# A hybrid state space and attention block: vector and scalar engine in program order through the state space stage

## The chip, the cores and the metric

One Trainium2 chip, one of its cores. The metric is the device time of one launch in microseconds (us), lower is better. The core's engines run side by side, each with a queue of its own: PE (TensorE, matmul; its weight loads are listed as PEld), DVE (VectorE), ACT (ScalarE), POOL (GpSimd) and SP (SyncE, which here only issues DMAs).

## The reference

One block on 512 tokens of width 1024, in float32:

```
proj = rms_norm(x) @ w_in
z, xbc, dt, q, k, v, g_ssd, g_attn = split(proj)
xbc = silu(causal_dwconv(xbc)); xs, B, C = split(xbc)       # 4 taps
# 8 groups of 4 heads of 64, state 128, chunks of 128 tokens:
y = (C B^T * decay) (xs dt) + C state_before_chunk * decay + d_skip * xs
y_ssd = rms_norm_by_group(y * silu(z))
y_attn = merge over 3 window groups by their softmax sums
merged = sigmoid(g_ssd) * (y_ssd @ w_ssd_proj) + sigmoid(g_attn) * (y_attn @ w_attn_proj)
x = x + merged @ w_out
x = x + (silu(u_gate) * u_val) @ w_down,   u = causal_dwconv(rms_norm(x) @ w_up)
```

## The kernel before

Every weight product runs in three float32r passes: the weight is split into `whi` (an ACT cast, L105) and `wlo` (a DVE subtraction, L106), the input into `hh` and `hl`, and a *piece* is 24 matmuls of 128x512 into one "mm" bank of PSUM: eight of whi·hh, eight of whi·hl, eight of wlo·hh (`mm_chan`, L140). `raw`, `whi` and `wlo` have three buffers each. PSUM has four "mm", two "tr" and two "aux" banks, each kind handed out in rotation (L61).

The stage in question has 48 pieces for the state space branch (`ps_ssd`), six for each of eight groups: B, C, two of xs, two of z; then 16 gate pieces (`ps_gate`). Between the pieces runs small work, held in *sides*: Python generators in a list (L121 to L138). A *tick* goes through the list, oldest first, and takes from each side the next portion, unless the side still waits: `yield n` means n ticks until the next portion. A piece has two ticks, one after its twelfth matmul (L148 to L150, behind a `prefetch` that makes the weight two pieces ahead) and one at its end (L815). So a group lasts twelve ticks. PE runs in the order in which the program issues (L152). For DVE and ACT, here, the framework chooses the order by a cost model of its own, and can place an instruction long before the tick that issues it. From the end of the output projection on (L1184) DVE, ACT and POOL too run in program order.

The sides are:

- `chain` (L525): attention, one per head pair, two per group of windows still running when the stage begins; the last ends at tick 9 and starts `combine` (L603), which waits eleven ticks. `combine` loads the softmax sums, forms weights `f`, transposes them (`ps_fT`, L626), copies them (`ft`, L628), sends them through DRAM, loads them back spread over partitions (`fb`), and then, for four head pairs j, does what is called a *strip* below: three products (L645) and two sums (L647) on DVE, a cast `ah` on ACT (L651), and a tick later `al` on DVE (L653).
- `conv4` (L676): the four-tap convolution of one piece out of its bank: one ACT step (L677) and three of DVE (L681, recorded as L51). It is called right after the piece, and so is the copy of z (L812).
- `silus` (L778): silu over a group's B and C, xs, or z.
- `ssd_side` (L696), one per group, with its waits from `G0`, `G1`, `GN`: the decay matrix `bc` (L705, L707, L708), the products C·B (`ps_cb`, L714, masked into `cbm`), B by token (`ps_bt`, L720, `btok`), `bc` times `cbm` (L723), xs by token (`ps_xt`, L733, twice four transposes) scaled into `xdt` and `xdc` (L736, L739), the chunk states (`ps_st`, L745) and their running sum `prev` (L750 to L754), and for each half j of the group's channels `ps_y` (L764), `ps_o` (L769) and four DVE steps that make y (L771 to L774). At its end it loads the decay of group g+2 (L685).

So PE meets a group's small matmuls in six portions: cb and bt, xt, xt, st, y and o of j = 0, y and o of j = 1. The gates' sigmoid (L836) is issued right behind its piece. Six early gates go to the buffers of the branch; `finish` (L842) runs the sides out, and POOL copies those gates into `gt` (L848), which lies where the sides' buffers were. Squares and norm sums of y follow among the gates (L856 to L876), then `normed` (L878).

## Time and profile before

| | us |
|---|---|
| median of 3 runs | 1191.93 (1191.52 to 1191.97) |
| the profiled execution | 1191.64 |
| its span, first to last instruction | 1189.9 |
| busy in it: PE, PEld | 1184.2, 988.0 |
| busy in it: DVE, ACT, POOL | 776.3, 574.5, 183.3 |

The profile is one execution. Times in its views run from the span's start; L12 is line 12 of the kernel. A row of a timeline gives start, duration, engine, line, operation, output and inputs, a count, and in brackets idle time with what ended it. A row of a list by lines gives busy time and the mean duration of one, then the idle time ahead of them. Matmuls are pipelined and their ends are modelled, so a matmul's cost is read from starts, not from durations. A busy PE is not a PE at its peak.

### The profile page before, as it was taken

What the parts mean: (1) busy time and instruction counts of PE and PEld (TensorE: products, weight loads), DVE (VectorE), ACT (ScalarE), POOL (GpSimd) and SP (SyncE); (2) the same over time, 40 slices, a digit from 0 to 9 for tenths busy, and PEclk for the clock granted to TensorE, in tenths of its full rate; (3) what the DMA queues carried; (4) which work ended last, traced back from release to release, by engine and by line L of the source; (5) the groups of instructions that cost most, each with busy time, mean ns of one, the idle gap of its engine ahead of it and who ended that gap; (6) DMA issues with size and microseconds to landing.
All of it is one profiled execution on the core that took longest, in us unless ns stands there. A gap on an engine that the chain in (4) does not pass through costs nothing.

```text
span 1189.9 us, 15865 instructions
## 1 busy us (share of the span) xinstructions
PE 1184.2 (100%) x6268; PEld 988.0 (83%) x6268; DVE 776.3 (65%) x1033; ACT 574.5 (48%) x870; POOL 183.3 (15%) x165
## 2 busy tenths in 40 slices
PE   9999999999999999999999999999999999999998
PEld 7877778987888888888887888888889898998887
DVE  6224454357789977767742374753779888888876
ACT  5434555467735655355325333432645454545443
POOL 1033432300000000000005400000133223222210
PEclk9999999999999999999999999999999999999999
DMA  5445543422645544425233523325434333249951
GB/s 189 124 112 127 127 109 91 108 55 76 183 136 176 145 124 124 142 72 142 71 85 79 173 98 100 90 89 193 143 105 125 89 107 106 80 132 279 189 123 66
DMA packets 175771, 145.24 MB, mean 122 GB/s; under 512 B 9752, under 2 KB 147848, under 8 KB 174673
## 3 DMA queue, kind: packets, MB, share of 16 engines
q1 hardware_dynamic: 167441, 127.11, 36.9%
q0 software_dynamic: 8256, 17.13, 7.3%
q8 instruction: 49, 0.80, 0.3%
q14 instruction: 25, 0.20, 0.1%
HBM read 139.51 MB, written 4.70 MB: 121 GB/s over the span
## 4 chain that ended last, share of the span: by engine, by line
PE 99%; ACT 0%; DVE 0%; issue 0%
PE ps_ssd L145 22%; PE ps_qk L145 11%; PE ps_u L1299 10%; PE ps_gate L145 7%; PE ps_sp L936 7%; PE ps_v L409 6%; PE ps_wo L969 3%; PE ps_dB L1500 3%; PE ps_ua L1125 2%; PE ps_uc L1125 2%; PE ps_ub L1125 2%; PE ps_u L145 2%; PE ps_da L1500 2%; PE ps_dc L1500 2%; PE ps_ap L145 2%; PE ps_s L537 1%
## 5 line engine op out<-in xcount | busy, mean ns | idle before, releaser
L106 DVE TENSOR_TENSOR wlo<-raw,whi 128x1024 fp32r<-128x1024 f32 x142 | 176.7, 1245 | 290.5 <-ACT whi L105 175.3
L105 ACT CAST whi<-raw 128x1024 fp32r<-128x1024 f32 x142 | 149.1, 1051 | 272.3 <-PE ps_ssd L145 75.4
L145 PE MATMUL ps_ssd<-hl,whi 128*128 128x512 f32 x384 | 102.4, 397 | 0.0
L145 PE MATMUL ps_ssd<-hh,whi 128*128 128x512 f32 x384 | 98.4, 398 | 0.0
L145 PE MATMUL ps_ssd<-hh,wlo 128*128 128x512 f32 x384 | 95.4, 390 | 0.0
L145 PEld LDWEIGHTS ps_ssd<-hh,wlo 128*128 128x128 f32 x384 | 72.1, 188 | 15.9
L145 PEld LDWEIGHTS ps_ssd<-hh,whi 128*128 128x128 f32 x384 | 70.6, 188 | 14.0 <-issue 0.2
L145 PEld LDWEIGHTS ps_ssd<-hl,whi 128*128 128x128 f32 x384 | 70.2, 188 | 13.8
L848 POOL COPY gt<-bct_gate 128x1024 f32<-128x1024 f32 x1 | 1.4, 1416 | 392.8 <-DVE ysb L773 392.8
L556 ACT ACTIVATE s<-s,st 128x128 f32<-128x128 f32 (+1 forms) x96 | 39.8, 416 | 21.6 <-DVE st L550 15.7
L1173 ACT ACTIVATE facc<-facc 128x512 f32<-128x512 f32 x22 | 13.9, 633 | 75.1 <-DVE facc L51 75.0
L145 PE MATMUL ps_qk<-hh,whi 128*128 128x512 f32 x192 | 49.3, 399 | 0.0
L1109 DVE TENSOR_TENSOR ulo<-rawup,uhi 128x1024 fp32r<-128x1024 f32 x31 | 44.6, 1437 | 5.2 <-ACT uhi L1103 5.2
L145 PE MATMUL ps_qk<-hl,whi 128*128 128x512 f32 x192 | 47.5, 389 | 0.0
L145 PE MATMUL ps_qk<-hh,wlo 128*128 128x512 f32 x192 | 47.4, 389 | 0.0
L145 PEld LDWEIGHTS ps_qk<-hh,whi 128*128 128x128 f32 x192 | 35.0, 188 | 12.1 <-issue 3.8
L1299 PE MATMUL ps_u<-h2h,uhi 128*128 128x512 f32 x176 | 43.7, 390 | 0.0
L1299 PE MATMUL ps_u<-h2l,uhi 128*128 128x512 f32 x176 | 43.5, 389 | 0.0
L1299 PE MATMUL ps_u<-h2h,ulo 128*128 128x512 f32 x176 | 43.4, 389 | 0.0
L145 PEld LDWEIGHTS ps_qk<-hl,whi 128*128 128x128 f32 x192 | 36.0, 188 | 7.6
L145 PEld LDWEIGHTS ps_qk<-hh,wlo 128*128 128x128 f32 x192 | 36.0, 188 | 7.5
L936 PE MATMUL ps_sp<-yh,whi 128*128 128x512 f32 x128 | 39.4, 389 | 0.0
(372 smaller groups left out, 2673.9 us busy)
## 6 DMA issues: line engine op xcount, KB each, us to landing
raw<-in_w_in_dram SPq DMA_DIRECT2D x100, 512.0 KB
rawup<-in_w_up_dram SPq DMA_DIRECT2D x40, 512.0 KB
bc<-scr_a SPq DMA_DIRECT2D x8, 1024.0 KB
raw<-in_w_ssd_proj_dram SPq DMA_DIRECT2D x16, 512.0 KB
c<-in_w_down_dram POOLq DMA_DIRECT2D x16, 512.0 KB, 6.3
hrb<-scr_q POOLq DMA_DIRECT2D x12, 512.0 KB, 6.5
raw<-in_w_down_dram SPq DMA_DIRECT2D x10, 512.0 KB
eb<-scr_e SPq DMA_DIRECT2D x16, 256.0 KB
```

Of the source, the lines that this page charges most:

```text
L105: nc.scalar.copy(hi, raw)
L106: marks["lo"] = nc.vector.tensor_sub(lo, raw, hi.bitcast(F32))
L145: nc.tensor.matmul(ps[:, t0:t0 + nt], a[:, k, c:c + n], b[:, k, t0:t0 + nt], start=(i == 0), stop=(i == total - 1))
L409: nc.tensor.matmul(pss[b], tok(g, kq * 2 + k, b, xx), w[:, k, :], start=(kq == 0 and j == 0 and k == 0), stop=(kq == 3 and j == 2 and k == 1))
L556: nc.scalar.activation(s[:, o:o + nk * P], s[:, o:o + nk * P], AF.Exp, bias=st[:, q, 0, 2 * j + h:2 * j + h + 1], accum_out=st[:, q, 1, 2 ...
L936: nc.tensor.matmul(pss[j], w[:, k, cs], ys[k][xi], start=(k2 == 0 and i == 0 and k == 0), stop=(k2 == 7 and i == 2 and k == 1))
L969: nc.tensor.matmul(pss[b], xs(k0 + k, i)[:, b * P:(b + 1) * P], ww[:, k, :], start=(k0 == 0 and j == 0 and k == 0), stop=(k0 == nk - 2 and ...
L1109: nc.vector.tensor_sub(lo, source(m, x), hi.bitcast(F32))
L1125: nc.tensor.matmul(ba[m][bk][:, c * H:(c + 1) * H], a[:, k, :], b[:, k, :], start=(i == 0), stop=(i == 11))
L1173: nc.scalar.activation(facc[m], facc[m], AF.Silu)
L1299: nc.tensor.matmul(pss[i], a[:, k, :], b[:, k, :], start=(n == 0), stop=(n == 23))
L1500: nc.tensor.matmul(ps, xs(j, q), w[wi][:, q, :], start=ps.name not in begun, stop=x in final and n == 5, skip_group_check=k in ("Q6", "Q3"))
```

## The change

DVE and ACT run in program order from the first state space piece to the end of the attention projection. With that the issuing program decides, and its order is written anew:

- `conv4`, the copy of z (now `keep_z`) and the sigmoid (now `sigmoid`) become sides: they begin with `yield 1` and so run at the middle of the next piece.
- `ssd_side` takes a table of the ticks of its steps, counted from the group's start: `GROUP`, and `FIRST` for group 0. `SILU` gives the ticks of the silus. A side's tick 12 is the first tick of the next group.
- A group's small matmuls go in three portions: `ps_bt`, both `ps_xt` and `ps_cb` (tick 13), `ps_st` (tick 17), `ps_y` and `ps_o` of both halves (tick 21). Their banks are four, two "tr" and two "aux". DVE and ACT work on them stands at ticks of its own. The decay of group g+2 is loaded ahead of the first half of y (tick 22).
- In `combine`, `ps_fT` takes an "mm" bank, and three ticks instead of one lie between `ah` and `al`, so a strip comes every four ticks instead of every two.
- `sq` holds one half instead of two, and `finish` is called once more after the gates.

```diff
-G0, G1, GN = (2, 1, 1, 1), (5, 2, 4, 2), (7, 2, 2)
-G2W, YL = 4, 3
+GROUP = (9, 11, 12, 13, 14, 15, 17, 18, 19, 21, 22, 23)
+FIRST = (12, 14, 15, 16, 17, 18, 19, 20, 21, 23, 24, 25)
+SILU = (8, 10, 14)
...
-        ps = bank("tr", "ps_fT")
+        ps = bank("mm", "ps_fT")
...
             nc.scalar.copy(ah[:, j, :], acc)
-            yield 1
+            yield 3
             nc.vector.tensor_sub(al[:, j, :], acc, ah[:, j, :].bitcast(F32))
...
+    ssd_cm = tc.manual_schedule(engines={mybir.EngineType.DVE, mybir.EngineType.Activation})
+    ssd_cm.__enter__()
...
     def conv4(ps, blk, acc):
+        yield 1
...
+    def keep_z(ps, o):
+        yield 1
+        nc.scalar.copy(o, ps)
...
+        waits = iter([b - a for a, b in zip(at, at[1:])])
...
         nc.vector.tensor_sub(m4, acs[:, :, hs]..., m4)
-        yield 1
+        yield next(waits)
         nc.scalar.activation(mt, mt, AF.Relu)
+        yield next(waits)
         nc.scalar.activation(mt, mt, AF.Exp, scale=-1.0)
-        yield at["cb"]
+        yield next(waits)
...
-        nc.scalar.copy(btok.rearrange("p c n -> p (c n)"), ps[:, :3 * P])
-        yield 1
-        nc.vector.tensor_mul(m4, m4, cbm.unsqueeze(1).broadcast_to((P, 4, NT, P)))
-        yield at["x"]
+        p4s = []
         for hf in range(2):
-            ps = bank("tr", f"ps_xt{g}_{hf}")
+            ps = bank(("tr", "aux")[hf], f"ps_xt{g}_{hf}")
...
+        psc = bank("aux", f"ps_cb{g}")
...
+        yield next(waits)
+        nc.scalar.copy(btok.rearrange("p c n -> p (c n)"), psb[:, :3 * P])
...
+            nc.vector.tensor_mul(xdc[:, cc], p4s[hf][:, :n], ...)
+        nc.vector.tensor_mul(cbm, psc..., triu...)
+        yield next(waits)
+            nc.vector.tensor_mul(xdt[:, cc], p4s[hf], ...)
+        yield next(waits)
...
+        yield next(waits)
+        nc.vector.tensor_mul(m4, m4, cbm.unsqueeze(1).broadcast_to((P, 4, NT, P)))
+        yield next(waits)
...
-        yield at["y"]
-        sq = T("sq", [P, 2, S])
+        yield next(waits)
+        outs = []
         for j in range(2):
-            psy = bank("aux", f"ps_y{g}_{j}")
+            psy = bank(("aux", "tr")[j], f"ps_y{g}_{j}")
...
-            pso = bank("aux", f"ps_o{g}_{j}")
+            pso = bank(("aux", "tr")[j], f"ps_o{g}_{j}")
...
+            outs.append((psy, pso))
+        sq = T("sq", [P, S])
+        for j in range(2):
+            yield next(waits)
+            if j == 0:
+                load_decay(g + 2)
...
-            yield YL - j
-        load_decay(g + 2)
...
-        if g > 1:
-            start(ssd_side(g, *tiles[g], normal), G2W if g == 2 else 0)
+            start(ssd_side(g, *tiles[g], GROUP), GROUP[0])
...
-                        conv4(banks[k], 16 + 8 * k + g, bct[:, k, :])
+                        start(conv4(banks[k], 16 + 8 * k + g, bct[:, k, :]))
...
-                        nc.scalar.copy(zs[:, k - 4, :], banks[k])
-            if i % 2 and g > 0:
-                start(silus(tiles[g][i // 2]), 1)
+                        start(keep_z(banks[k], zs[:, k - 4, :]))
+            if i % 2:
+                start(silus(tiles[g][i // 2]), SILU[i // 2] - 2 * i - 1)
...
-                start(ssd_side(0, *tiles[0], dict(zip(("cb", "x", "y"), G0))), G0[3])
-            if (g, i) == (0, 5):
-                start(ssd_side(1, *branch_tiles(1), dict(zip(("cb", "x", "y"), G1))), G1[3])
-                start(silus(*tiles[0]), 1)
+                start(ssd_side(0, *tiles[0], FIRST), FIRST[0] - 10)
+    def sigmoid(ps, o):
+        yield 1
+        nc.scalar.activation(o, ps, AF.Sigmoid)
...
-        nc.scalar.activation(o, ps, AF.Sigmoid)
+        start(sigmoid(ps, o))
         tick()
...
+    finish()
...
     nl_cm.__exit__(None, None, None)
+    ssd_cm.__exit__(None, None, None)
```

## The prediction

> **What bounds the kernel now.** The page comes first: who holds the chain of waits, and at what clock.

> ```profile
> PE 99%; ACT 0%; DVE 0%; issue 0%
> ```

> ```profile
> core 0 of [0], span 1189.9 us
> core 0: us, PE busy (x) PEld busy (x) DVE busy (x) ACT busy (x) POOL busy (x), PEclk, DMA share, GB/s
> 373.00:393.00 20.00, 20.00 (x103) 16.39 (x102) 19.75 (x33) 9.09 (x12) 0.00 (x0) 1.00 0.62 185
> 513.00:553.00 40.00, 40.00 (x215) 33.00 (x214) 29.23 (x38) 19.95 (x21) 0.00 (x0) 1.00 0.43 118
> ```

> The chain is TensorE from end to end. In both windows, which lie in the stage that changes, PE is busy throughout and the granted clock is 1.00. So the change can win only what PE itself spends, and every wait that it adds to PE is paid in full. Two windows matter: a steady group (513 to 553) leaves DVE a quarter of its time, while the stretch 373 to 393, where the merging of the three attention groups (`combine`) runs beside groups 1 and 2, fills DVE to 19.75 of 20 us. Today the scheduler spreads that work; afterwards the program does.

> Next, what PE spends on a group's small work: the timeline of PE in a steady group.

> ```profile
> 454.68 1.07 PE L145 MATMUL ps_ssd<-hl,whi 128*128 128x512 f32 x4
> 455.67 1.09 PE L764 MATMUL ps_y<-bc,xdt 128*64 128x128 f32 x16
> 456.70 0.94 PE L769 MATMUL ps_o<-bct,prev 128*128 128x128 f32 x6
> 457.39 1.17 PE L145 MATMUL ps_ssd<-hl,whi 128*128 128x512 f32 x4
> ```

> ```profile
> 462.05 1.07 PE L145 MATMUL ps_ssd<-hl,whi 128*128 128x512 f32 x4
> 462.96 1.05 PE L714 MATMUL ps_cb<-bct 128*128 128x128 f32 x8
> 463.85 0.49 PE L720 MATMUL ps_bt<-ident,bct 128*128 128x128 f32 x3
> 464.09 1.17 PE L145 MATMUL ps_ssd<-hl,whi 128*128 128x512 f32 x4
> 465.11 1.99 PE L145 MATMUL ps_ssd<-hh,wlo 128*128 128x512 f32 x8
> ```

> ```profile
> 478.78 1.46 PE L745 MATMUL ps_st<-xdc,btok 128*128 128x256 f32 x6
> 479.89 2.19 PE L145 MATMUL ps_ssd<-hh,whi 128*128 128x512 f32 x8
> ```

> Read by starts. Four piece matmuls take 0.91 us (462.05 to 462.96), 0.227 each, so a piece of 24 takes 5.44 and the half between two ticks 2.72. From 462.05 to 465.11 pass 3.06 us, of which eight piece matmuls are 1.81: the portion cb+bt costs 1.25. Its eight `ps_cb` step by 0.11 (0.89 in all), and eleven records at that step are 1.22. Going over to small matmuls and back thus costs about 0.03. The portion y+o costs 454.68 to 457.39 less 0.91, 1.80, and 0.11 for the slow four behind it (1.02 for 0.91 at 464.09): 1.9. It begins 0.08 late (455.67 for 455.59), a price of entering. The portion st costs 1.11, with its restart 1.2.

> **The change, part by part.**

> Fewer portions. A group has six today (cb+bt, two of four transposes, st, two of y+o) and then three, with the same matmuls: bt, both transposes and cb together (19 records by 0.11, 2.15 us), st, and both halves of y+o (3.8). Three borders go. At 0.03 each that is 0.1 us a group, 0.8 in all; with the entry of 0.08 saved each time too, 0.33 and 2.6. I take 1.0, near the low end, because the entry into the narrow `ps_y` tiles comes back inside the merged portion, from `ps_o` to the second `ps_y`. **Term one: minus 1.0 us (0.8 to 2.6).**

> Program order on DVE and ACT. The prices, one steady group first, then the strip of `combine` and the way that DVE instructions overlap:

> ```profile
> L106 DVE TENSOR_TENSOR wlo<-raw,whi 128x1024 fp32r<-128x1024 f32 x6 | 7.3, 1222 | 6.2 <-PE ps_ssd L145 4.4 <-ACT whi L105 1.8
> L51 DVE SCALAR_TENSOR_TENSOR xst<-ps_ssd,sc,xst 128x511 f32<-128x511 f32 (+2 forms) x6 | 4.5, 744 | 0.1
> ...
> L723 DVE TENSOR_TENSOR bc<-bc,cbm 128x2048 f32<-128x2048 f32 x1 | 2.3, 2283 | 0.0
> ...
> L51 DVE SCALAR_TENSOR_TENSOR ysb<-xst,dsk,ps_y 128x512 f32<-128x512 f32 x2 | 1.5, 744 | 0.2 <-PE ps_y L764 0.2
> L774 DVE TENSOR_TENSOR ysb<-ysb,zs 128x512 f32<-128x512 f32 x2 | 1.4, 692 | 0.1
> L736 DVE TENSOR_TENSOR xdt<-ps_xt,dtt 128x512 f32<-128x512 f32 x2 | 1.4, 692 | 4.0 <-PE ps_xt L733 4.0
> L773 DVE TENSOR_TENSOR ysb<-ysb,sq 128x384 f32<-128x384 f32 x2 | 1.1, 554 | 0.0
> L772 DVE TENSOR_TENSOR sq<-ps_o,eb 128x384 f32<-128x384 f32 x2 | 1.1, 553 | 0.1
> L739 DVE TENSOR_TENSOR xdc<-ps_xt,dtd 128x512 f32<-128x512 f32 (+1 forms) x2 | 1.1, 546 | 0.0
> L752 DVE TENSOR_TENSOR prev<-prev,cdec 128x256 f32<-128x256 f32 x2 | 0.8, 420 | 0.0
> ```

> ```profile
> L645 DVE TENSOR_TENSOR ysb<-ysb,fb 128x512 f32<-128x512 f32 x8 | 5.1, 682 | 0.0
> ```

> ```profile
> 605.96 1.23 DVE L106 TENSOR_TENSOR wlo<-raw,whi 128x1024 fp32r<-128x1024 f32 x1 [3.30 <-PE ps_gate L145]
> 607.10 0.74 DVE L51 SCALAR_TENSOR_TENSOR ysb<-xst,dsk,ps_y 128x512 f32<-128x512 f32 x1
> ```

> ```profile
> L105 ACT CAST whi<-raw 128x1024 fp32r<-128x1024 f32 x7 | 7.3, 1042 | 10.0 <-PE ps_ssd L145 10.0
> ...
> L708 ACT ACTIVATE bc<-bc 128x2048 f32<-128x2048 f32 x1 | 1.9, 1917 | 0.0
> L677 ACT ACTIVATE xst<-ps_ssd,sc 128x512 f32<-128x512 f32 x2 | 1.6, 781 | 1.6 <-PE ps_ssd L145 1.6
> ...
> L708 ACT ACT_TABLE_LOAD x1 | 1.3, 1283 | 0.0
> L812 ACT COPY zs<-ps_ssd 128x512 f32<-128x512 f32 x2 | 1.2, 576 | 0.0
> ```

> The next DVE instruction starts 1.14 us after a `wlo` of 1.23, so I take 0.09 off each that waits for nothing: `wlo` 1.14, a convolution (three of L51) 1.97, the `bc` products 2.2, a `combine` operation 0.60, so a strip (three products, two sums) 3.0 and its `al` 0.6. Chains whose members wait for each other keep full length: a half of y 2.5, `prev` (five of 0.42) 2.1.

> A steady group has room. Its tightest place is the wait of y+o (tick 21) for `prev` (tick 19): from tick 18 DVE does `wlo`, the `bc` product, a convolution and `prev`, 7.4 us, and PE takes 2.72 and 5.44, 8.2. Cost nothing; each us beyond that margin of 0.8 would cost one us in each of six groups.

> Ticks are counted from here on from group 0's first piece; group 1 begins at 12, group 2 at 24. `combine`, which wakes at tick 21, makes `ps_fT` and `ft` at 24 (after yields of 1 and 2) and its first strip at 28 (2 and 2 more).

> Ticks 24 and 25, the middle and the end of a piece. At tick 24 the oldest side, `combine`, puts its `ft` copy into DVE's queue ahead of group 0's y; `ft` waits for PE's `ps_fT`. Let group 0's y+o start on PE at 0. PE: 3.8, half a piece 2.72, four transposes 0.44, half a piece 2.72: at 9.7 it wants group 1's first portion, whose two "tr" banks hold y's second half. DVE: `ft` can start at 7.1, takes 0.6, y's first half 2.5, the first read of the second 0.74: 10.9. **Term two: plus 1.2 us**; with `ft` behind y it would be 0.

> Ticks 28 to 45: strips stand at ticks 28, 32, 36 and 40, each with an ACT copy (`ah`) that waits for it, and behind that copy ACT's convolution, silu, exp or cast, for which DVE's next instruction waits. At tick 28 DVE starts level with PE (its `wlo` needs the buffer that PE frees just then). Up to tick 35 it has five `wlo` 5.7, three convolutions 5.9, two strips 6.0, two `al` 1.2, two `bc` products 4.4, `prev` 2.1, two y halves 5.0, together 30.3, and it waits behind `ah`: once for `ah`, priced like the z copy, and the convolution's first step (0.58, 0.78, so 1.3), once for these and a silu as long as a cast (2.3). Sum 33.9. PE needs 4.5 pieces 24.5, st 1.2, y+o 3.8: 29.5. DVE is 4.4 behind at tick 36. There it does a strip (3.0), and then ACT works alone: `ah` 0.58, table load 1.28, exp 1.92, z copy 0.58, cast 1.04, 5.1 with overlaps. Only then come `wlo` 1.14, two `xdc` and `cbm` 1.5, a wait of 0.7 for ACT's table load, silu and convolution, the convolution 1.97, `al` 0.6, two `xdt` 1.2: 7.1. In all 19.6 after tick 36. PE wants group 2's st (tick 41), whose bank the second `xdt` frees, after 2.72, the first portion 2.15 and two pieces 10.88, at 15.75. **Term three: plus 3.8 us.** From there to y+o at tick 45 DVE has 1.14, 3.0, 1.3, 1.97, 1.14, 2.2, 1.97, 0.6, 2.1: 15.4; PE 1.2 and 10.88: 12.1. **Term four: plus 3.3.** Afterwards no strip is left, and DVE's quarter of spare time clears the rest.

> Bounds of these three: without overlap (0.09 on some 35 instructions) 3 us more; if the ACT-alone waits (1.3, 2.3, 5.1) were half as long, 4.3 less.

> [...]

> The rest at nothing. `ps_fT` in an "mm" bank and the later reading of banks: four banks, a bank returns three pieces (16 us) later. Later silus, sigmoids and `al`: `merged` is read only after the last gate. The loads of decay are issued at tick 22 and used eleven ticks on; on SP's queue they can hold back weight loads, of which three buffers lie ahead: 0, at worst 2 us. POOL's copies of the early gates:

> ```profile
> 619.25 1.42 POOL L848 COPY gt<-bct_gate 128x1024 f32<-128x1024 f32 x1 [392.78 <-DVE ysb L773]
> ```

> ```profile
> 632.19 1.53 POOL L848 COPY gt<-zs_gate 128x1024 f32<-128x1024 f32 x1 [9.35 <-ACT zs_gate L836]
> ```

> Their release, group 7's last y, comes some ten us later, about 629, and the third copy waits for its sigmoid until 632 anyway; beyond that the norm sums on PE would wait one for one.

> **Sum.** The profiled execution took 1191.64 us, its span 1189.9 and 1.7 around it, 0.3 below the median 1191.93. 1191.64 − 1.0 + 1.2 + 3.8 + 3.3 = 1198.9 us.

> **Rivals.** *No new wait (1190.6, not slower).* PE stays gapless and only term one is left. For it: today's trace does the same DVE work in 373 to 393 without a PE gap. Against: there strips slip in between other work; in program order each strip's `ah` holds ACT. It holds if DVE is under 0.5 us behind at tick 36. Chance 0.22. *One stall only (about 1193.5):* DVE starts tick 28 ahead, or the 5.1 overlap with work; terms two and a part of three remain, plus 1 to 3. Chance 0.15. *Faster (1188.5):* all borders are worth 0.4 us a group, 8 × 0.4 = 3.2; it needs the merged portion to shed entry, exit and the step from y to o as well. Chance 0.06. *A tax in every group (1205):* the margin of 0.8 is gone, say 1 us in six groups on top of the forecast; the steady group's 29.23 of 40 speaks against it. Chance 0.07. That DVE and ACT are not held to program order would look like the first.

> **Numbers.** Forecast (1195 to 1203) 0.50. From 1190.2 to 1203 lie the forecast, the single stall and most of the first rival, 0.83. A measurement of this kernel tells 0.2%, 2.4 us, from no change: faster 0.06, same 0.30 (the first rival and half of the single stall), slower 0.64.

> **What would show it.** Right: three PE gaps in the new trace, before group 1's `ps_bt`, group 2's `ps_st` and group 2's first `ps_y`, each ended by DVE (y, `xdt`, `prev`); ACT `ah` waiting 5 us and more for DVE; DVE `wlo` waiting some 5 us for ACT `whi` near tick 38; a steady group shorter by 0.1. Wrong: a gapless PE, or gaps in every group.

## The result and the profile after

The changed kernel takes 1208.69 us (median of 5 runs) where the kernel before took 1191.53 beside it: 17.2 us more, a ratio of 1.0143 (95% interval 1.0127 to 1.0159). The forecast was slower, 1198.9 us, with a range up to 1203.0: the sign was right, the size was not. One of the five executions, the profiled one, ran at a granted clock of 0.56 and took 1976.28 us (the median of the other four is 1208.5), so the profile read here is of the same kernel run again (1207.72 us, span 1206.0, clock 0.997; median of its four executions 1209.25).

The page's chain of waits, which was PE at 99% before:

```profile
PE 39%; ACT 0%; DVE 0%; issue 0%
```

It is followed back from the end and covers only the last 39% of the span: in order of time its first entry stands at 724.97 us. From there on PE is the bound; what broke it lies ahead. The windows of three stretches (the columns are busy us and instructions by engine, then granted clock and DMA):

```profile
345.00:440.00 95.00, 86.44 (x473) 70.30 (x473) 77.61 (x117) 44.51 (x49) 0.00 (x0) 0.98 0.51 141
473.00:513.00 40.00, 40.00 (x215) 33.27 (x214) 29.91 (x39) 20.18 (x21) 0.00 (x0) 1.00 0.42 120
700.00:750.00 50.00, 47.05 (x197) 37.87 (x196) 28.50 (x38) 16.08 (x23) 0.00 (x0) 0.97 0.26 84
```

and the first of them in the kernel before:

```profile
345.00:440.00 95.00, 95.00 (x514) 78.30 (x512) 82.46 (x113) 48.46 (x51) 0.00 (x0) 1.00 0.57 161
```

In the first, PE idles 8.6 us of 95, and DVE is *less* busy than before (77.61 for 82.46): DVE isn't full, it waits. A steady group (the second) is as gapless as before. The third window, at the start of the output projection, was in no part of the prediction. The timeline of PE, its waits in brackets:

```profile
357.94 0.52 PE L726 MATMUL ps_bt<-ident,bct 128*128 128x128 f32 x3 [1.19 <-DVE ysb L55]
...
398.70 0.52 PE L726 MATMUL ps_bt<-ident,bct 128*128 128x128 f32 x3 [0.55 <-DVE ysb L55]
...
412.97 1.10 PE L760 MATMUL ps_st<-xdc,btok 128*128 128x256 f32 x4 [0.92 <-DVE cbm L749]
417.65 1.15 PE L760 MATMUL ps_st<-xdc,btok 128*128 128x256 f32 x2 [3.58 <-DVE xdt L754]
418.24 3.56 PE L149 MATMUL ps_ssd<-hh,whi 128*128 128x512 f32 x8
421.63 2.02 PE L149 MATMUL ps_ssd<-hl,whi 128*128 128x512 f32 x8
...
433.23 1.09 PE L780 MATMUL ps_y<-bc,xdt 128*64 128x128 f32 x16 [2.32 <-DVE prev L772]
```

Three gaps stand where the prediction put them, ended by what it named (y, `xdt`, `prev`), and a fourth, small one at 398.70. Behind the gap at 417.65 eight matmuls take 3.39 us to the next row (418.24 to 421.63) instead of 1.81: half clock. The chain of causes on the other engines, by the view of the waits between 345 and 440 us (total us, times, the longest):

```profile
ACT ah L655 <- DVE ysb L651: 30.7, 4, 9.6
DVE wlo L110 <- ACT whi L109: 9.4, 2, 5.3
...
ACT f L617 <- DVE f L616: 4.8, 1, 4.8
```

And the timeline of ACT at the worst place, tick 36, with DVE's next instruction in the fence behind it:

```profile
404.76 0.62 ACT L655 CAST ah<-ysb 128x512 fp32r<-128x512 f32 x1 [8.16 <-DVE ysb L651]
405.40 1.28 ACT L721 ACT_TABLE_LOAD   x1
406.70 1.92 ACT L721 ACTIVATE bc<-bc 128x2048 f32<-128x2048 f32 x1
408.52 0.57 ACT L692 COPY zs<-ps_ssd 128x512 f32<-128x512 f32 x1
408.98 1.05 ACT L109 CAST whi<-raw 128x1024 fp32r<-128x1024 f32 x1
```

```profile
401.39 1.29 DVE L649 TENSOR_TENSOR ysb<-ysb,fb 128x512 f32<-128x512 f32 x2
...
410.06 1.22 DVE L110 TENSOR_TENSOR wlo<-raw,whi 128x1024 fp32r<-128x1024 f32 x1 [5.33 <-ACT whi L109]
```

ACT stands 8.16 us behind `ah` while table load, exp, z copy and cast, none of which need the strip, queue behind it; then they run alone and DVE stands 5.33 us behind the cast. Each engine waits in its turn for the other.

The start of the output projection: PE, ACT and DVE of this kernel, then ACT and DVE of the kernel before:

```profile
721.33 1.02 PE L960 MATMUL ps_sp<-yh,whi 128*128 128x512 f32 x2 [0.75 <-ACT yh L943]
724.41 1.40 PE L960 MATMUL ps_sp<-yl,whi 128*128 128x512 f32 x2 [2.06 <-DVE yl L944]
```

```profile
719.71 1.05 ACT L109 CAST whi<-raw 128x1024 fp32r<-128x1024 f32 x1 [4.38 <-PE ps_ap L149]
720.66 3.21 ACT L943 CAST yh<-ysb 128x512 fp32r<-128x512 f32 x6
```

```profile
723.67 3.69 DVE L944 TENSOR_TENSOR yl<-ysb,yh 128x512 fp32r<-128x512 f32 x6
```

```profile
699.31 1.66 ACT L919 CAST yh<-ysb 128x512 fp32r<-128x512 f32 x3
703.79 1.06 ACT L105 CAST whi<-raw 128x1024 fp32r<-128x1024 f32 x1 [2.83 <-PE ps_ap L145]
704.76 1.65 ACT L919 CAST yh<-ysb 128x512 fp32r<-128x512 f32 x3
```

```profile
702.92 1.89 DVE L920 TENSOR_TENSOR yl<-ysb,yh 128x512 fp32r<-128x512 f32 x3
```

Before, the framework placed the splits `yh` and `yl` of the output projection between the pieces of the attention projection, where ACT idles. Now they all come behind the end of program order, which the change put behind the attention projection: the six `yh` start at 720.66, when PE has just run out of work, and the six `yl` at 723.67.

### The profile page after: what moved, and what is told of

It reads as the page before. It is cut to its first block, busy times and chain, and to the rows that moved or that the text cites. A ratio compares the mean times of both kernels' runs of the same rounds, so it can differ in the third digit from the quotient of the medians.

```text
span 1974.6 us, 15883 instructions
## 1 busy us (share of the span) xinstructions
PE 1967.0 (100%) x6268; PEld 1231.9 (62%) x6268; DVE 777.9 (39%) x1033; ACT 577.2 (29%) x870; POOL 169.9 (9%) x165
## 5 line engine op out<-in xcount | busy, mean ns | idle before, releaser
L149 PE MATMUL ps_ssd<-hh,whi 128*128 128x512 f32 x384 | 161.6, 588 | 0.0
L149 PE MATMUL ps_ssd<-hl,whi 128*128 128x512 f32 x384 | 158.7, 576 | 0.0
L149 PE MATMUL ps_ssd<-hh,wlo 128*128 128x512 f32 x384 | 157.1, 578 | 0.0
L149 PE MATMUL ps_qk<-hl,whi 128*128 128x512 f32 x192 | 78.6, 577 | 0.0
L149 PE MATMUL ps_qk<-hh,whi 128*128 128x512 f32 x192 | 78.5, 575 | 0.0
L149 PE MATMUL ps_qk<-hh,wlo 128*128 128x512 f32 x192 | 78.5, 577 | 0.0
L1323 PE MATMUL ps_u<-h2h,ulo 128*128 128x512 f32 x176 | 71.8, 576 | 0.0
L960 PE MATMUL ps_sp<-yl,whi 128*128 128x512 f32 x128 | 61.9, 580 | 2.6 <-DVE yl L944 2.6
L960 PE MATMUL ps_sp<-yh,wlo 128*128 128x512 f32 x128 | 61.6, 576 | 0.0
L1323 PEld LDWEIGHTS ps_u<-h2l,uhi 128*128 128x128 f32 x176 | 38.9, 221 | 28.6 <-issue 15.7
```

What stands on the lines that cost most here:

```text
L149: nc.tensor.matmul(ps[:, t0:t0 + nt], a[:, k, c:c + n], b[:, k, t0:t0 + nt], start=(i == 0), stop=(i == total - 1))
L960: nc.tensor.matmul(pss[j], w[:, k, cs], ys[k][xi], start=(k2 == 0 and i == 0 and k == 0), stop=(k2 == 7 and i == 2 and k == 1))
L1323: nc.tensor.matmul(pss[i], a[:, k, :], b[:, k, :], start=(n == 0), stop=(n == 23))
```

## The experiments

Times are medians; the kernel before took 1191.5 to 1191.7 beside each.

**Program order taken away.** The lines that enter and leave program order left out, all else as changed.

> The changed program with the two lines left out that hold DVE and ACT to program order, so the framework orders them again; portions, tables of ticks, deferred convolutions and banks stay as in the change. Theory A and B (program order makes the waits): 1189 to 1192 us, a PE without gaps and a clock of 1.00. Rival C (the larger portions or their four banks make the waits, whoever orders DVE and ACT): 1200 to 1209 us.

1190.29 us, ratio 0.9989 (0.9979 to 0.9998), PE gapless, clock 1.00. So program order makes all of the loss, and the rest of the change, above all the new portions, gains 1.4 us. It also gives an unstalled trace of the same program to compare with.

**The changed kernel again**, for the profile above.

> The changed kernel as it is, for a profile at the full clock. Theory A (stalls that also cost clock): its profile shows the three PE gaps of the prediction, together 7 to 9 us, and behind each gap a stretch with a granted clock below 1.00; the missing clock is worth 6 to 9 us more. Theory B (more waits than forecast): PE gaps add up to 15 us or more, some of them outside groups 1 and 2 (every group, the gates, the output projection), and the clock costs under 2 us.

Matmul by matmul (the same one of each tile in both traces, the difference of their starts), the 17.5 us between the spans 1206.0 and 1188.5 fall to these places:

| place | stall, us | half clock behind it, us |
|---|---|---|
| in group 0, beside the last attention chains (294) | 0.4 | |
| before group 1's ps_bt (term two) | 1.5 | |
| before group 2's ps_bt | 0.9 | |
| before and in group 2's ps_st (term three) | 5.3 | 1.4 |
| before group 2's ps_y (term four) | 2.4 | |
| start of the output projection | 3.3 | 2.2 |

A stall here includes the slow first matmuls behind it. The gaps alone are 1.35 us before group 1's ps_bt, 0.71 before group 2's, 4.82 at its ps_st, 2.39 before its ps_y, and 0.91 and 2.34 at the output projection; the texts below use these.

Neither theory has the numbers. The stalls, 13.8 us, lie between the two; two of them (294 and the output projection) are outside groups 1 and 2, as B had it; and the clock costs 3.6 us, more than B's 2 and less than A's 6 to 9. What stands at 294 stays, at 0.2 to 0.4, in every version with program order, and was followed no further.

**`ah` later.**

```diff
-            nc.scalar.copy(ah[:, j, :], acc)
-            yield 3
+            yield 2
+            nc.scalar.copy(ah[:, j, :], acc)
+            yield 1
```

> The changed kernel with the cast `ah` of a strip issued two ticks after the strip instead of right behind it, one tick ahead of `al`; DVE has the same work in the same order. Theory A (ACT stands still behind `ah`, and so does DVE, which waits for ACT): DVE's waits of 1.36, 2.31, 5.33, 0.66 and 1.36 us go, and with them the PE gaps of 0.71, 4.82 and 2.39 us and the stretch at half clock behind the second (1.4 us): about 1199.5 us. Rival D (DVE simply has more work there than fits in program order, whatever ACT does): it stays late, the gaps before group 2's ps_st and ps_y shrink by less than half: 1204 us or more.

1198.06 us, 11.2 less than the 1209.25 of the changed kernel. The windows of this version:

```profile
395.00:440.00 45.00, 45.00 (x247) 37.78 (x246) 41.44 (x56) 24.83 (x27) 0.00 (x0) 1.00 0.51 145
700.00:730.00 30.00, 27.16 (x106) 21.27 (x105) 19.06 (x26) 9.41 (x14) 0.00 (x0) 0.89 0.28 91
```

PE is busy all 45 us of group 2, with DVE's work and order untouched. The rival (too much work for DVE) is out. Left are the gap before group 1's ps_bt (1.35) and the output projection.

**Program order for one engine alone.**

```diff
-    ssd_cm = tc.manual_schedule(engines={mybir.EngineType.DVE, mybir.EngineType.Activation})
+    ssd_cm = tc.manual_schedule(engines={mybir.EngineType.DVE})
```

> The changed kernel with DVE alone held to program order; the framework orders ACT. Theory A: ACT takes what is ready ahead of `ah`, DVE no longer waits for it, and group 2's gaps go; `ft` still stands ahead of y (1.5 us or less) and yl still stands behind the last norm (up to 5.5 us): 1195 to 1198.5 us. Rival D (DVE has too much work there for any program order): 1204 us or more.

> The changed kernel with ACT alone held to program order; the framework orders DVE. Theory A (the loss needs both: DVE waits in its order for ACT, which waits in its order for DVE): with DVE free the strip that ACT waits for can come earlier or other work before it, so most of the loss in the group stage goes; yh is still held back by ACT's order at the output projection, at most 5.5 us: 1191 to 1197 us. Rival H (ACT's order by itself makes the loss): 1203 us or more.

DVE alone: 1197.7 us; the group stage keeps only the 1.35 before group 1's ps_bt, and the output projection stalls as before. ACT alone: 1190.92 us, ratio 0.9993 (0.9984 to 1.0002), and no new gap over 0.3 us; rival H is out. ACT still waits 20.3 us for the four strips there, but with DVE free no wait of PE comes of it. Group 2's stalls need both queues in program order; for the output projection DVE's is enough. Theory A had `yh` held back by ACT's order; that was wrong. With ACT alone in program order the `yh` lie between the pieces again (699.04 and 704.48), and with DVE alone all six start at 710.66, behind its end, though ACT is free. Why DVE's order holds back a cast on ACT isn't shown.

**One `ah` of four later** (the third, tick 36).

```diff
+            if j == 2:
+                yield 2
             nc.scalar.copy(ah[:, j, :], acc)
-            yield 3
+            yield 1 if j == 2 else 3
```

> The changed kernel with only the third of the four casts `ah` (tick 36, the one ahead of group 2's relu, table load and exp on ACT) issued two ticks later; the other three stay behind their strips. Theory A: DVE's wait of 5.33 us for the cast `whi` goes, and with it the gap of 4.82 us before and in group 2's ps_st and the half clock behind it; the 0.71 before ps_bt stays, and the gap before ps_y (2.39) shrinks by at most 1: 1201 to 1203 us. Rival G (every `ah` costs alike, a quarter of the 11.2 us that all four together cost): 1206.4 us.

1205.32 us: neither number. DVE's wait of 5.33 went and group 2's ps_st came without a gap, as theory A said, but the next gap did not shrink, it grew:

```profile
411.82 1.83 PE L762 MATMUL ps_st<-xdc,btok 128*128 128x256 f32 x6
...
428.52 1.76 PE L782 MATMUL ps_y<-bc,xdt 128*64 128x128 f32 x14 [3.95 <-DVE prev L774]
```

2.39 became 4.0, with 2.6 us of half clock behind it. (The profile, of an execution of 1204.07 us, has no half clock at the output projection, where the changed kernel lost 2.2; so here the gaps say more than the time.) A stall of PE is also the time in which DVE catches up; without the one at ps_st DVE arrived later, measured against PE, at ps_y. A stall taken away is only gained if DVE's lag goes with it.

**Program order ended after the last gate.**

```diff
             normed(2 * (m - 14) + 1)
     finish()
+    ssd_cm.__exit__(None, None, None)
...
     nl_cm.__exit__(None, None, None)
-    ssd_cm.__exit__(None, None, None)
```

> The changed kernel with program order ended after the last gate instead of after the attention projection, so the framework again orders DVE and ACT from there and can place the splits yh and yl of the output projection between the attention projection's pieces. Theory A: the two waits of PE at the start of the output projection (0.91 and 2.34 us) and the half clock behind them (2.2 us) go: about 1203.8 us. Rival E (the splits are late because the norms of y are late, whatever the order): unchanged, 1208 to 1209 us.

1203.01 us, 6.2 less, and the start of the output projection is full again. Rival E is out. In the profiled execution (1203.55) it is 4.2 less: the stall before group 2's ps_y, which the early end doesn't touch, was now followed by half clock worth 1.6 us (the last section says why).

```profile
700.00:730.00 30.00, 30.00 (x134) 24.83 (x133) 20.48 (x29) 10.03 (x14) 0.00 (x0) 1.00 0.28 89
```

**`ft` behind y.**

```diff
+        yield 2
         ft = comb.tile([24, S], F32, tag="ft", name="ft")
         nc.vector.tensor_copy(ft, ps[:24, :])
         nc.sync.dma_start(scr_f, ft)
-        yield 2
```

> The changed kernel with the copy `ft` two ticks after its transposes instead of right behind them, so that group 0's y stands ahead of it on DVE; the strips stay at their ticks. Theory A (term two): the gap of 1.35 us before group 1's ps_bt goes, 1207.7 us; DVE is then ahead at tick 28 by as much, so the gaps at group 2 may shrink a little too, 1206 to 1207.7 us. Rival F (the gap is y's own length on DVE, not ft): the gap stays at 0.7 us or more, 1208.5 to 1209.3 us.

1207.9 us. Between the two theories: the gap shrank from 1.35 to 0.63. The timeline of DVE in this version shows what is left:

```profile
353.19 1.23 DVE L110 TENSOR_TENSOR wlo<-raw,whi 128x1024 fp32r<-128x1024 f32 x1 [4.03 <-ACT whi L109]
354.33 0.74 DVE L55 SCALAR_TENSOR_TENSOR ysb<-xst,dsk,ps_y 128x512 f32<-128x512 f32 x1
```

y could not start earlier because the `wlo` ahead of it waited for ACT, and ACT had stood 4.8 us behind the exponential of `f` (the third row of the waits): the same pattern as `ah`. But `ft` alone is enough for the whole gap. With DVE alone in program order that `wlo` starts at 349.99, without a wait for ACT; `ft` waits for PE, y starts at 354.53 behind it, and the gap is 1.35 all the same. From the waits of that version:

```profile
DVE ft L632 <- PE ps_fT L630: 2.7, 1, 2.7
```

So the two causes overlap, and the wait for ACT shows only when `ft` is out of the way.

**The three together, and a fourth edit** that issues that exponential a tick after its inputs:

```diff
             nc.vector.tensor_sub(f[:, :, g, :], mx, st[:, :, g, 0, :])
+        yield 1
         nc.scalar.activation(f, f, AF.Exp)
...
-        yield 2
+        yield 1
         ps = bank("mm", "ps_fT")
```

> The three edits together (late `ah`, early end of program order, `ft` behind y). Theory A: no PE gap is left that the kernel before does not have, clock 1.00, and the time is that of the version whose order is free, 1190.3 us (1189.8 to 1191). If some of the loss lies elsewhere in program order (the steady groups, queues), 1192 to 1196 us.

> The version with three edits (1191.92 us) and a fourth: in the merging of the attention groups the exponential of the weights `f` is issued one tick after the subtractions that it needs, so ACT does not stand 4.8 us behind it with group 1's relu and the next cast waiting, and DVE not 4.0 us behind that cast. Theory A: the gap of 0.63 us that is left before group 1's ps_bt goes, with 0.26 of waits around it: 1190.3 to 1191.1 us. Rival (y's two halves are too long for DVE in that place, whatever ACT does): unchanged, 1191.9 us.

1191.92 us with three, ratio 1.0003 (0.9994 to 1.0012): between theory A's number and the other, for the gap of 0.63 stayed, and one of 0.25 before group 2's ps_y. With four, 1190.72, 0.9992 (0.9983 to 1.0001), and both are gone. The fourth edit did more than it was meant to: ACT's wait for `f` only fell from 4.8 to 3.35 us, but a silu now ran ahead of it, and two table loads of 1.28 us fell away (between 340 and 354 us three edits have three of them, four edits one); DVE's wait for `whi` fell from 4.03 to 1.18. Which of these closed the gap isn't separated. So the loss is accounted for: it lay at four places, three in the issue order and one at the end of the stretch, and not in program order as such. The version with four edits cannot be told from the kernel before; of all versions only the free order is (barely) faster.

**Waits of set length**, in the version with four edits: ahead of ps_st of groups 3 to 6, nothing left out.

```diff
+        if 3 <= g <= 6:
+            dly = T("dly", [P, S])
+            nc.scalar.copy(dly, banks[-1])
+            for _ in range((3, 5, 7, 9)[g - 3]):
+                nc.scalar.copy(btok, btok)
```

> The version with four edits, and in it PE is made to wait before ps_st of groups 3, 4, 5 and 6: ACT first copies out of the bank of the piece that PE has just ended, then copies btok onto itself 3, 5, 7 and 9 times, and ps_st waits for that. One copy takes 0.57, the others 0.48 each, so PE should wait about 2.2, 3.1, 4.1 and 5.0 us, 40 us apart. [...]

1215.3 us (two executions, 1214.8 and 1215.8): 24.6 more than without. By the starts of the matmuls the waits are 2.33, 3.42, 4.50 and 5.59 us, together 15.8, and half clock costs another 1.7, 1.7, 2.7 and 2.5 behind them. The waits came a little above their forecast (2.2, 3.1, 4.1 and 5.0), and the shortest, 2.33 us, was already followed by half clock. The last section says with what that went.

## Why the prediction was too low

*Term one, minus 1.0:* right; free order measures 1.4. From one ps_y to that of the next group PE now takes 39.89 us (473.11 to 513.00); before it was 40.06 (455.67 in the prediction's rows, to 495.73). 0.17 a group is 1.4 for eight, inside the 0.8 to 2.6.

```profile
473.11 1.09 PE L780 MATMUL ps_y<-bc,xdt 128*64 128x128 f32 x16
...
513.00 1.09 PE L780 MATMUL ps_y<-bc,xdt 128*64 128x128 f32 x16
```

```profile
495.73 1.09 PE L764 MATMUL ps_y<-bc,xdt 128*64 128x128 f32 x16
```

*Term two, 1.2:* 1.5 measured; the place, the releaser and the reason were right, for `ft` ahead of y makes the whole gap even when ACT is free. But the claim that it would be 0 with `ft` behind y was not: 0.63 stayed, because ACT behind `f` is a second cause.

*Term three, 3.8:* 0.9 and 5.3. The mechanism was right, and so were the waits behind `ah` (1.3 and 2.3 forecast, 1.36 and 2.31 measured; 5.1 forecast, 5.33 measured). Mis-sized was DVE's own time: from the `wlo` of tick 28 to the strip of tick 36 the trace of DVE has

```profile
365.93 1.23 DVE L110 TENSOR_TENSOR wlo<-raw,whi 128x1024 fp32r<-128x1024 f32 x1 [0.27 <-issue]
...
371.78 2.32 DVE L55 SCALAR_TENSOR_TENSOR bct<-ps_ssd,sc,bct 128x511 f32<-128x511 f32 x3 [1.36 <-ACT bct L684]
374.01 1.21 DVE L110 TENSOR_TENSOR wlo<-raw,whi 128x1024 fp32r<-128x1024 f32 x1
...
401.39 1.29 DVE L649 TENSOR_TENSOR ysb<-ysb,fb 128x512 f32<-128x512 f32 x2
```

35.5 us where the sum had 33.9. A convolution takes 2.23 (371.78 to 374.01, three of 0.74), not 1.97, for its three members wait for each other: they should have kept full length by the prediction's own rule. Three convolutions make 0.8, two strips at 3.35 (401.39 to ACT's `ah` at 404.76) for 3.0 make 0.7. DVE came to tick 36 about 6 us late instead of 4.4, and everything behind it shifted. The lag showed first at group 2's ps_bt, a gap that the prediction did not have.

*Term four, 3.3:* 2.4; the half clock of PE behind the stall before it gave DVE 1.4 us to catch up.

*"The rest at nothing"* is the step that failed. The prediction went through the work inside program order and left out what had been placed across its end, so the sum has no term for the output projection. The splits `yh` and `yl` are not touched by the diff, but they had run inside the stretch that the change closed. Their coming late cost 3.3 us of stalls and 2.2 of half clock: 5.5 of the 8.8 us by which the profiled execution lies above the forecast (9.8 for the median). The mis-sized term three (2.4 more) and the half clock at group 2 (1.4) come next. The rows that show where they ran were in the trace of before (699.31 and 704.76 above).

*The clock*, set at nothing in the sum: 1.4 at group 2 and 2.2 at the output projection. Between its matmuls PE never idled longer than 0.57 us in the trace of before (ahead of 842.13), so that trace could not show what a longer idle costs.

Sum: 7.3 forecast; 0.3 more in term two, 2.4 in term three with its two gaps, 0.9 less in term four, 0.4 more gain in term one, 1.4 of clock, 5.5 at the output projection, 0.4 at 294: 16.0. The two profiled executions differ by 1207.72 − 1191.64 = 16.1. The medians differ by a further 1 or so: the other three executions of the profiled run granted a clock of 0.994 for its 0.997, and took 0.8 to 2.6 us more. The range ended at 1203.0 and left out a further stall elsewhere; the rival nearest in size (a tax in every group, 1205) had the wrong place, for the steady groups lost nothing.

## What to carry to other kernels

When two engines that feed each other are put into program order, look in each queue for an instruction that is issued right behind a long job of the other engine: everything behind it stands still, and then the other engine does (8.16 us on ACT and 5.33 on DVE here). Issue the consumer a step after its producer; here three such moves, and an earlier end of program order, took the kernel from 1209.25 to 1190.72 us with the same work. At both ends of a stretch of program order, look for what was placed across that border before, and count a stall of PE at its length and what half clock may add behind it: in these runs 1.4 to 2.7 us behind stalls of some 2.3 us and more, and nothing behind one of 2.39.

## What the runs showed of the hardware

```profile
449.84:453.25 3.41, 1.24 (x6) 1.00 0.00 0
453.25:456.66 3.41, 3.41 (x10) 0.50 0.25 57
```

```profile
414.34:417.75 3.41, 0.10 (x1) 1.00 0.04 13
417.75:421.16 3.41, 3.41 (x9) 0.50 0.33 85
...
431.40:434.82 3.42, 1.59 (x21) 1.00 0.00 0
...
434.82:438.23 3.41, 3.41 (x32) 1.00 0.50 133
```

```profile
430.76:434.17 3.41, 1.09 (x17) 1.00 0.00 0
```

PE busy for 1.24 of 3.41 us: the next stretch is at half clock. Busy for 1.59, in the wait before ps_y that ends at 433.23: the next one is at full clock. So a wait of 2.33 us lost 1.7 us more, and one of 2.39 nothing, by where each lay. The wait before ps_y in the version with the early end, at the same place of the program and about as long, left 1.09 us busy in its stretch, and the next one, from 434.17, was at half clock. Across these runs the border for a stall at full clock lies between 1.41 us of busy time (411.78 to 415.19 in the version with `ft` behind y, half clock next) and the 1.59 above, but for one stretch of 1.94 (709.51 to 712.92) in the version with the later `ah`, which was followed by half clock too. Busy time is a rough measure here, for the ends of matmuls are modelled; that stretch isn't explained.
